# Up phase of a Strassen ConvFFN: weights in four places per pair, another product order, and the down weights' sums spread over all pairs

## The chip, the cores and the metric

One core of one Trainium2 chip runs the whole program. The metric is the device time of one execution in microseconds (us). TensorE (PE) multiplies, VectorE (DVE), ScalarE (ACT) and GpSimd (POOL) do the elementwise work, and SyncE (SP) issues nearly all transfers of the part that is changed, in program order.

## The reference

A decoder layer: three attention branches, a gated merge, and then a gated ConvFFN, which is where the change lies. All matrices are float32.

```
x = x + conv_ffn(rms_norm(x, norm2_g[l]), w_up[l], conv_w[l], conv_b[l], w_down[l])

def conv_ffn(h, w_up, conv_w, conv_b, w_down):
    a, b = jnp.split(h @ w_up, 2, axis=-1)
    a = lax.conv_general_dilated(a, conv_w..., padding=[(CONV_WIDTH - 1, 0)], ...) + conv_b
    return (jax.nn.gelu(a) * b) @ w_down
```

The sizes are: sequence 1024, model width 1024, D_FF 2816, so h @ w_up is 1024x1024 by 1024x5632, and the second product is 1024x2816 by 2816x1024.

## The kernel before

Both products of the ConvFFN are done with one level of the Strassen-Winograd scheme: a 2x2 block product in seven block products instead of eight, paid for with sums of the blocks. A product of fp32 accuracy is made of three matmuls (`mm3`: high by high on L283, low by high on L284, high by low on L285), so every operand is split into a rounded high part (a cast on ACT) and the rest (a subtraction on DVE).

**Up phase** (`ffn`). The 5632 columns are worked in 22 pairs s = 0 to 21; pair s takes 128 columns of the half a and the 128 columns of the half b that belong to them. The weights of a pair are four blocks of 128x512 elements: A11 and A12 (columns of a, upper and lower half of the rows), A21 and A22 (columns of b). A pair has seven products of 12 matmuls each, 84 matmuls of 128x512 (pair 0 has eight plain products; pair 1 has its own order, `EARLY`; all others go by `PRODUCTS`). Three sums of weights are made in place as soon as a pair's product S2 is prepared: su = A21 + A22 (L1400), S3 = A11 - A21 (L1402), S2 = su - A11 (L1404); S4 (L1407) follows later. They run on POOL, for pairs 0 and 1 on DVE. `prep` makes the sum if one is due, casts to the high part on ACT (L1411) and takes the low part on DVE (L1412; on POOL for pairs 0 and 1). Products are prepared three ahead (AHEAD) into a ring of four buffers ("wh" and "wl" in turn, two each). Every result comes out of PSUM through an add on DVE, goes through the convolution (`conv`: ACT L1465, two DVE steps L1470, ACT L1471) and is gated (`gated`, DVE L1475), and `left` and `sums` store the seven left operands of the second product to DRAM (L1430, L1440).

`load` brings a pair's weights as two transfers of 512 KB (L1384), one with A11 and A12, one with A21 and A22, into three buffers in rotation (two "wr", one "fr"). A buffer is free when every block in it, sums included, has been split.

`down_weights(k)`, for k = 0 to 10, is independent of all that: two loads of w_down (L1420, 512 KB each), four sums on POOL (L1421 to L1424) and two stores (L1426), in buffers "t2" that nothing else uses at that point. In the program it stands in pairs 1, 3, 5, ...; the scheduler of the framework sorts each engine's instructions by when their inputs are ready.

**Down phase** (`ffn_down`). Seven products of 11 blocks each; a block n is two loads (L1584, L1590), a cast of 128x1024 on ACT (L1592), a subtraction on DVE (L1593) and 12 matmuls. Blocks are loaded four ahead. Two of five blocks go through buffers of the long-lived pool wp, three of five through the pool dp. dp lies where the buffers of the up phase were, so its first loads wait until the last stores of the up phase have read theirs.

Of the kernel before, what the change touches and what calls it, by code (L numbers as in the profile page):

```python
# [13 lines left out]
P = 128  # L14
# [216 lines left out]
class Trunk:  # L231
# [1072 lines left out]
    PRODUCTS = (("A11", "B11"), ("S2", "T2"), ("A12", "B21"), ("S3", "T3"), ("A22", "T4"), ("S1", "T1"), ("S4", "B22"))  # L1304
# [62 lines left out]
    def ffn(self, np_, x1, B, blks):  # L1367
# [7 lines left out]
        cnt = {"raw": 0, "op": 0}  # L1375
        v, g = nc.vector.tensor_tensor, nc.gpsimd.tensor_tensor

        def load(s):
            pair, j = [], order[s]
            for c0 in (j * P, DFF + j * P):  # L1380
                pool, tag = (fp, "fr") if cnt["raw"] % 3 == 2 else (wp, "wr")
                cnt["raw"] += 1
                r = pool.tile([P, 8, P], F32, tag)
                nc.sync.dma_start(r, wup[:, c0:c0 + P].rearrange("(k p) n -> p k n", p=P))  # L1384
                pair.append(r)
            raws[s] = {"A11": pair[0][:, 0:4], "A12": pair[0][:, 4:8], "A21": pair[1][:, 0:4], "A22": pair[1][:, 4:8]}
# [4 lines left out]
        def prep(s, i):  # L1391

            if i == 0 and 0 < s < NF - 1:
                load(s + 1)
            q = raws[s]
            name = names(s)[i]
            e = g if s > 1 else v
            if name == ("S1" if s == 1 else "S2"):
                s1 = fp.tile([P, 4, P], F32, "su")
                e(s1, q["A21"], q["A22"], ALU.add)  # L1400
                q["S1"] = s1
                e(q["A21"], q["A11"], q["A21"], ALU.subtract)  # L1402
                q["S3"] = q["A21"]
                e(q["A11"], s1, q["A11"], ALU.subtract)  # L1404
                q["S2"] = q["A11"]
            if name == "S4":
                e(q["A12"], q["A12"], q["S2"], ALU.subtract)  # L1407
                q["S4"] = q["A12"]
            o = wp.tile([P, 2, 4, P], F32R, ("wh", "wl")[cnt["op"] % 2])
            cnt["op"] += 1  # L1410
            nc.scalar.copy(o[:, 0], q[name])  # L1411
            (v if s > 1 else g)(o[:, 1], q[name], o[:, 0].bitcast(F32), ALU.subtract)  # L1412
            ops[s, i] = o

        def down_weights(k):

            w = [np_.tile([P, 2, 512], F32, "t2") for _ in range(2)]
            for x in range(2):
                r = (k + x * NH) * P
                nc.sync.dma_start(w[x], wdn[r:r + P].rearrange("p (n c) -> p n c", n=2))  # L1420
            g(w[0][:, 1], w[0][:, 1], w[0][:, 0], ALU.subtract)  # L1421
            g(w[1][:, 1], w[1][:, 1], w[0][:, 1], ALU.subtract)
            g(w[0][:, 0], w[1][:, 1], w[0][:, 0], ALU.subtract)
            g(w[1][:, 0], w[1][:, 0], w[1][:, 1], ALU.subtract)  # L1424
            for x in range(2):
                nc.sync.dma_start(dt[k][:, 2 * x:2 * x + 2], w[x])  # L1426
# [22 lines left out]
        fp = Pool(self, "ffn", {"t1": 2})  # L1449
        load(1)  # L1450
        AHEAD = 3
        for s in range(NF):
# [51 lines left out]
            for i, (an, bn) in enumerate(self.EARLY if s == 1 else self.PRODUCTS):  # L1504
# [5 lines left out]
                if s % 2 == 1 and i == 4:  # L1510
                    down_weights(s // 2)
# [7 lines left out]
                elif s == 1:  # L1519
# [11 lines left out]
                    elif an == "S3":  # L1531
                        add(p1, p1)
                    else:
                        add(u2, p1)
                        gated(0, u2)
                        v(p1, p1, u3, ALU.add)
                        gated(1, p1)
                elif an == "S2":
                    add(u2, p1)
                elif an == "A12":  # L1540
                    add(p1, p1)
                    conv(0, p1)
                elif an == "S3":
                    add(u3, u2)
                elif an == "A22":
                    add(p1, u3)
                    gated(0, p1)
                elif an == "S1":
                    add(u2, u2)
                    add(u3, u3)  # L1550
                else:
                    add(u2, u2)
                    conv(1, u2)
                    gated(1, u3)
        sums(NH - 1)
        fp.close()
        np_.close()
        for p in blks:
            p.close()
        self.ffn_down(x1, dl, dt)  # L1560

    def ffn_down(self, x1, dl, dt):
# [4 lines left out]
        dp = Pool(self, "down", {"wr": 3, "wh": 3, "wl": 3, "st": 4})  # L1567
        rp = Pool(self, "downr", {"hi": NH, "lo": NH}, side="right")
        U = rp.tile([P, 4, 512], F32, "U")
        V = rp.tile([P, 4, 512], F32, "V")  # L1570
        fg = rp.tile([P, D], F32, "fg")
        nc.sync.dma_start(fg, a["final_g"].rearrange("(o d) -> o d", o=1).to_broadcast([P, D]))
        cnt = [0]

        def ring():
            cnt[0] += 1
            return wp if cnt[0] % 5 in (1, 2) else dp

        def operands(p, k, keep=None):

            an, bn = self.DOWN[p]
            pool = ring()
# [8 lines left out]
            hi, lo = ((keep or pool).tile([P, 2, 512], F32R, n) for n in (("hi", "lo") if keep else ("wh", "wl")))  # L1591
# [34 lines left out]
        ops = {n: operands(*seq[n]) for n in range(AHEAD)}  # L1626
        lasts = []
        lo_, hi_ = slice(0, 512), slice(512, 1024)
        for p in range(6):
            ps = [self.bank_tile() for _ in range(4)]  # L1630
            for k in range(NH):
                n = p * NH + k
                if n + AHEAD < len(seq):
                    ops[n + AHEAD] = operands(*seq[n + AHEAD])
# [3 lines left out]
                for t in range(4):  # L1638
                    step(ps[t], o, t, k == 0, k == NH - 1)
            for t in range(4):  # L1640
# [153 lines left out]
```

## Time and profile before

| What | Value |
|---|---|
| median of 3 runs | 1839.32 us (1835.39 to 1840.0) |
| profiled execution, its own time | 1841.05 us |
| span of that execution | 1839.3 us |
| mean granted clock of PE | 0.975 |
| PE busy | 1711.3 us (93%), 8600 matmuls |
| DVE busy | 1205.0 us (66%) |
| ACT busy | 770.8 us (42%) |
| POOL busy | 397.0 us (22%) |

The span is what the profiler saw of the program; the execution's own time lies 1.75 us above it. Matmuls are pipelined and their busy times overlap, so a PE that is shown busy is not yet at its best pace; the distance between starts tells the pace. The change touches the last third of the span.

### The profile page before, as it was taken

The numbers are of one execution on the slowest core, as the hardware profiler recorded it, in microseconds if no ns is written. First come the engines' busy times: TensorE is split into PE (matmuls) and PEld (weight loads), VectorE is DVE, ScalarE is ACT, GpSimd is POOL, SyncE is SP. The second block draws the span as 40 slices with busy tenths as digits, with TensorE's granted clock in tenths as the row PEclk, the third lists the DMA queues.
The fourth block names the chain that finished last, engine by engine and source line by source line (L and its number), as shares of the span: only waits on it lengthen the run. The fifth ranks groups of instructions, "written<-read, shape, count | busy, mean of one in ns | idle before, by whom it ended". The sixth has DMA issues, their size and how long they took to land. (4 is left out here: it accounts for less than half of the span.)

```text
span 1839.3 us, 24513 instructions
## 1 busy us (share of the span) xinstructions
PE 1711.3 (93%) x8600; PEld 1406.3 (76%) x8600; DVE 1205.0 (66%) x2518; ACT 770.8 (42%) x1572; POOL 397.0 (22%) x295
## 2 busy tenths in 40 slices
PE   7999999879899999999999997887999999879998
PEld 6888887768687888888877875666777777658876
DVE  7366676645567775666487179686868777745764
ACT  5335555432454534555554134222333333334452
POOL 4311101002111111111133207666332223100000
PEclk9999999989999999999999998998999999989999
DMA  8756566677425273221565402575532232467662
GB/s 256 205 138 159 145 155 181 159 197 199 111 77 157 70 183 93 77 64 47 187 202 193 152 4 83 177 235 174 182 96 87 93 108 86 130 214 229 211 208 74
DMA packets 223329, 266.49 MB, mean 145 GB/s; under 512 B 19720, under 2 KB 159086, under 8 KB 222998
## 3 DMA queue, kind: packets, MB, share of 16 engines
q1 hardware_dynamic: 214550, 246.94, 45.5%
q10 hardware_dynamic: 8208, 15.21, 2.3%
q0 software_dynamic: 448, 2.78, 0.4%
q8 instruction: 68, 1.11, 0.2%
q14 instruction: 55, 0.45, 0.1%
HBM read 187.23 MB, written 80.36 MB: 145 GB/s over the span
## 5 line engine op out<-in xcount | busy, mean ns | idle before, releaser
L283 PE MATMUL dn<-hTh,wh 128*128 128x512 f32 x704 | 285.7, 406 | 2.1 <-DVE sl L488 2.1
L285 PE MATMUL dn<-hTh,wl 128*128 128x512 f32 x704 | 277.3, 394 | 0.0
L284 PE MATMUL dn<-hTl,wh 128*128 128x512 f32 x704 | 276.9, 393 | 0.0
L271 POOL TENSOR_TENSOR wl<-wr,wh 128x1024 fp32r<-128x1024 f32 (+2 forms) x60 | 112.7, 1878 | 700.7 <-ACT wh L269 621.6
L712 ACT ACTIVATE p<-S,sm 128x384 f32<-128x384 f32 (+2 forms) x192 | 106.5, 559 | 138.3 <-DVE sm L708 103.8
L285 PEld LDWEIGHTS dn<-hTh,wl 128*128 128x128 f32 x704 | 133.1, 189 | 29.3
L283 PEld LDWEIGHTS dn<-hTh,wh 128*128 128x128 f32 x704 | 134.2, 191 | 20.8 <-DVE sl L488 2.5
L284 PEld LDWEIGHTS dn<-hTl,wh 128*128 128x128 f32 x704 | 134.0, 190 | 19.0
L776 DVE TENSOR_TENSOR tl<-T,th 128x512 fp32r<-128x512 f32 (+2 forms) x202 | 115.5, 585 | 33.9 <-ACT th L775 32.9
L704 DVE TENSOR_REDUCE sm<-S 128x1 f32<-128x384 f32 (+2 forms) x192 | 96.2, 525 | 52.6 <-PE S L701 51.7
L775 ACT CAST th<-T 128x512 fp32r<-128x512 f32 (+2 forms) x202 | 99.6, 510 | 67.5 <-PE T L769 64.7
L1593 DVE TENSOR_TENSOR wl<-wr,wh 128x1024 fp32r<-128x1024 f32 x66 | 80.2, 1223 | 63.0 <-ACT wh L1592 60.7
L701 PE MATMUL S<-k,q 114*128 114x384 f32 (+6 forms) x240 | 95.5, 398 | 16.3 <-issue 7.7
L1592 ACT CAST wh<-wr 128x1024 fp32r<-128x1024 f32 x66 | 69.3, 1053 | 95.8 <-PE dn L285 61.9
L798 PE MATMUL PV<-th,v 128*128 128x256 f32 (+1 forms) x362 | 94.0, 285 | 4.5 <-DVE yt L815 4.0
L769 PE MATMUL T<-ident,p 128*128 128x128 f32 x610 | 93.7, 275 | 2.2 <-DVE tl L776 2.1
L799 PE MATMUL PV<-tl,v 128*128 128x256 f32 (+1 forms) x362 | 89.3, 283 | 2.6 <-DVE tl L776 2.6
L697 PE MATMUL S<-k,q 128*128 128x384 f32 (+2 forms) x240 | 84.1, 350 | 6.8 <-DMA k<-dk_b 4.5
L769 PEld LDWEIGHTS T<-ident,p 128*128 128x128 f32 x610 | 72.8, 141 | 15.0 <-DVE tl L776 3.1
L798 PEld LDWEIGHTS PV<-th,v 128*128 128x128 f32 x362 | 69.1, 191 | 9.7 <-DVE yt L815 6.4
L799 PEld LDWEIGHTS PV<-tl,v 128*128 128x128 f32 x362 | 69.6, 192 | 6.2 <-DVE tl L776 3.7
L283 PE MATMUL S<-blk,wl 128*128 128x512 f32 x152 | 62.0, 408 | 12.2 <-ACT wl L1411 12.2
(463 smaller groups left out, 4451.4 us busy)
## 6 DMA issues: line engine op xcount, KB each, us to landing
wr<-w_in SPq DMA_DIRECT2D x44, 512.0 KB
wr<-dl SPq DMA_DIRECT2D x77, 256.0 KB
wr<-w_up SPq DMA_DIRECT2D x30, 512.0 KB
dg<-f ACTq DMA_DIRECT2D x48, 256.0 KB
gr<-dg SPq DMA_DIRECT2D x24, 512.0 KB
t<-w_down SPq DMA_DIRECT2D x22, 512.0 KB
dt<-t SPq DMA_DIRECT2D x22, 512.0 KB
wr<-dt SPq DMA_DIRECT2D x44, 256.0 KB
```

The lines of the kernel that those rows point to most:

```text
L271: eng.tensor_tensor(lo, raw, hi.bitcast(F32), ALU.subtract)
L283: nc.tensor.matmul(out, st[0], mv[0], start=first, stop=False)
L284: nc.tensor.matmul(out, st[0], mv[1], start=False, stop=False)
L285: nc.tensor.matmul(out, st[1], mv[0], start=False, stop=last)
L701: nc.tensor.matmul(ps[:, 0:wn * P], q[1][0:R, qs], k[1][0:R, cs], start=False, stop=True)
L704: nc.vector.tensor_reduce(mx if ci == 0 else sm[:, 1:2], v, AX.X, ALU.max, negate=True)
L712: nc.scalar.activation(pt[:, 0:m, :].rearrange("p a b -> p (a b)"), v, AF.Exp, bias=mx, accum_out=sm[:, 2 + ci:3 + ci])
L769: nc.tensor.transpose(ps[:, n * P:(n + 1) * P], b, self.ident)
L775: nc.scalar.copy(th[:, cs], ps[:, cs])
L776: nc.vector.tensor_tensor(tl[:, cs], ps[:, cs], th[:, cs].bitcast(F32), ALU.subtract)
L798: nc.tensor.matmul(unit.pv[:, oc], w, th[:, cs], start=first and i == 0, stop=False)
L799: nc.tensor.matmul(unit.pv[:, oc], w, tl[:, cs], start=False, stop=e)
```

## The change

The four weight blocks of a pair get places of their own. A11 and A12 have two sets of places in turn (half of the first "wr" buffer each for even pairs, half of "fr" each for odd pairs); A21 and A22 have one set (the second "wr" buffer) for all pairs. A load now brings one block (256 KB), so there are 88 loads of w_up instead of 44. A11 and A12 of the next pair are asked for when a pair's first product is prepared, A21 as soon as S3 (which sits in A21's place) is split, A22 as soon as A22 is split. The order of the products becomes A11, A12, S2, S3, A22, S1, S4 (A12 and S2 change places), and the partial results of a pair change tiles: what u3 held is in p1 and the reverse. `down_weights` stands in pairs 2, 3, 5, 6, 8, 10, 11, 13, 14, 16 and 18, and its two loads are tied to come after the last load of w_up that was issued before them. In the down phase, blocks 0 to 3 go through wp (block 2's split parts through "t2" buffers) before the buffers of the up phase are given up; blocks 4 to 7 are prepared at n = 3 instead of one at a time at n = 0 to 3; final_g is loaded into a tile made at n = 12.

```diff
-    PRODUCTS = (("A11", "B11"), ("S2", "T2"), ("A12", "B21"), ("S3", "T3"), ("A22", "T4"), ("S1", "T1"), ("S4", "B22"))
+    PRODUCTS = (("A11", "B11"), ("A12", "B21"), ("S2", "T2"), ("S3", "T3"), ("A22", "T4"), ("S1", "T1"), ("S4", "B22"))
...
-        def load(s):
-            pair, j = [], order[s]
-            for c0 in (j * P, DFF + j * P):
-                pool, tag = (fp, "fr") if cnt["raw"] % 3 == 2 else (wp, "wr")
-                cnt["raw"] += 1
-                r = pool.tile([P, 8, P], F32, tag)
-                nc.sync.dma_start(r, wup[:, c0:c0 + P].rearrange("(k p) n -> p k n", p=P))
...
+        place = lambda t, x: t[:, x * 4:x * 4 + 4]
+        raw = [wp.tile([P, 8, P], F32, "wr") for _ in range(2)]
+        SLOTS = {("A11", 0): place(raw[0], 0), ("A12", 0): place(raw[0], 1), ("A21", 0): place(raw[1], 0),
+                 ("A22", 0): place(raw[1], 1)}
+
+        def load(s, what=("A11", "A12", "A21", "A22")):
+            q = raws.setdefault(s, {})
+            for n in what:
+                r = q[n] = SLOTS[n, s % 2 if n[1] == "1" else 0]
+                k0, c0 = (512 if n[2] == "2" else 0), order[s] * P + (DFF if n[1] == "2" else 0)
+                self.upload = nc.sync.dma_start(r, wup[k0:k0 + 512, c0:c0 + P].rearrange("(k p) n -> p k n", p=P))
...
             if i == 0 and 0 < s < NF - 1:
-                load(s + 1)
+                load(s + 1, ("A11", "A12"))
...
             ops[s, i] = o
+            if 0 < s < NF - 1 and name in ("S3", "A22"):
+                load(s + 1, ("A21",) if name == "S3" else ("A22",))
...
-                nc.sync.dma_start(w[x], wdn[r:r + P].rearrange("p (n c) -> p n c", n=2))
+                with self.tc.issue_after(self.upload.ins):
+                    nc.sync.dma_start(w[x], wdn[r:r + P].rearrange("p (n c) -> p n c", n=2))
...
+        raw.append(fp.tile([P, 8, P], F32, "fr"))
+        SLOTS.update({("A11", 1): place(raw[2], 0), ("A12", 1): place(raw[2], 1)})
...
+        DOWN_AT = [2 + (8 * k) // 5 for k in range(NH)]
...
-                if s % 2 == 1 and i == 4:
-                    down_weights(s // 2)
+                if i == 4 and s in DOWN_AT:
+                    down_weights(DOWN_AT.index(s))
...
-            return wp if cnt[0] % 5 in (1, 2) else dp
+            return wp if cnt[0] % 5 in (4, 0) else dp
...
-            pool = ring()
+            pool = ring() if dp else wp
...
-        ops = {n: operands(*seq[n]) for n in range(AHEAD)}
+
+        ops = {n: operands(*seq[n], first=np_ if n == 2 else None) for n in range(AHEAD)}
...
-                if n + AHEAD < len(seq):
-                    ops[n + AHEAD] = operands(*seq[n + AHEAD])
+                if n >= 3:
+                    for m in range(max(AHEAD, n + 1 if n == 3 else n + AHEAD), min(n + AHEAD, len(seq) - 1) + 1):
+                        ops[m] = operands(*seq[m])
...
+                if n == 2:
+                    np_.close()
+                    for x in blks:
+                        x.close()
+                    dp = Pool(self, "down", {"wr": 3, "wh": 3, "wl": 3, "st": 4})
...
+                if n == 12:
+                    fg = rp.tile([P, D], F32, "fg")
+                    nc.sync.dma_start(fg, a["final_g"].rearrange("(o d) -> o d", o=1).to_broadcast([P, D]))
```

In the changed file the lines move: the weight sums are L1403, L1405, L1407 and L1410, the low part is L1415, the loads of w_up L1389, the down weights' loads, sums and stores L1426, L1427 to L1430 and L1432, the stores of left operands L1436 and L1446, the down phase's loads L1585 and L1591 and that of final_g L1654.

The first place is POOL in pair 1, where it makes the low parts (L1412) of that pair's products. Before:

```order
L1421 TENSOR_TENSOR t_2435_12058<-t_2435_12058 128x512
L1422 TENSOR_TENSOR t_2436_12059<-t_2436_12059,t_2435_12058 128x512
L1423 TENSOR_TENSOR t_2435_12058<-t_2436_12059,t_2435_12058 128x512
L1424 TENSOR_TENSOR t_2436_12059<-t_2436_12059 128x512
L1412 TENSOR_TENSOR wl_11962<-fr_11824,wl_11962 128x512
L1412 TENSOR_TENSOR wh_11969<-su_11965,wh_11969 128x512
L1412 TENSOR_TENSOR wl_11977<-fr_11824,wl_11977 128x512
```

And of the change at the same place:

```order
L1415 TENSOR_TENSOR wl_11963<-fr_11826,wl_11963 128x512
L1415 TENSOR_TENSOR wh_11970<-su_11966,wh_11970 128x512
L1415 TENSOR_TENSOR wl_11978<-fr_11826,wl_11978 128x512
L1415 TENSOR_TENSOR wh_11995<-fr_11826,wh_11995 128x512
L1415 TENSOR_TENSOR wl_12018<-wr_11518,wl_12018 128x512
L1415 TENSOR_TENSOR wh_12036<-wr_11518,wh_12036 128x512
L1403 TENSOR_TENSOR su_12096<-wr_11518 128x512
```

The four sums of down_weights(0) no longer stand ahead of pair 1's low parts; the first set on POOL now comes after pair 3's first three weight sums.

The second place is SP in the middle of the up phase, around one set of down weights. Before (an early stretch, with pair 3 at work: the second load of pair 4, the first of pair 5, and the down weights k = 4 and 5):

```order
L1420 DMA t_2631_13311<-w_down 128x1024
L1420 DMA t_2632_13312<-w_down 128x1024
L1384 DMA wr_12220<-w_up 128x8x128
L1426 DMA dt_2349_11510<-t_2631_13311 128x1024
L1426 DMA dt_2349_11510<-t_2632_13312 128x1024
L1384 DMA wr_12365<-w_up 128x8x128
L1420 DMA t_2680_13624<-w_down 128x1024
L1420 DMA t_2681_13625<-w_down 128x1024
```

And of the change, around the set k = 6, which stands in pair 11 (wr_11518 is the second "wr" buffer, with A21 and A22; fr_11826 and wr_11517 are the two sets of places of A11 and A12):

```order
L1389 DMA wr_11518<-w_up 128x4x128
L1389 DMA fr_11826<-w_up 128x4x128
L1389 DMA wr_11518<-w_up 128x4x128
L1389 DMA fr_11826<-w_up 128x4x128
L1426 DMA t_2657_13635<-w_down 128x1024
L1426 DMA t_2658_13636<-w_down 128x1024
L1436 DMA dl_2339_11500<-gb_13552 128x512
L1432 DMA dt_2351_11512<-t_2657_13635 128x1024
L1432 DMA dt_2351_11512<-t_2658_13636 128x1024
L1389 DMA wr_11517<-w_up 128x4x128
L1389 DMA wr_11518<-w_up 128x4x128 x2
```

The loads of the down weights are now behind A21 and A22 of pair 12 and A11 and A12 of pair 13, and their two stores stand ahead of A11 of pair 14 and of A21 and A22 of pair 13.

The third place is SP where the up phase hands over to the down phase. Before (blocks k of the left operands are dl_2334 for k = 0 to dl_2344 for k = 10):

```order
L1584 DMA wr_15396<-dl_2334_11495 128x512
L1430 DMA dl_2344_11505<-x_15102 128x512
L1430 DMA dl_2344_11505<-tt_15240 128x512
L1590 DMA wr_15396<-dt_2345_11506 128x512
L1584 DMA wr_15415<-dl_2344_11505 128x512
L1440 DMA dl_2344_11505<-gb_14951 128x1024
L1430 DMA dl_2344_11505<-x_15102 128x512
L1590 DMA wr_15415<-w_down 128x512
L1584 DMA wr_15491<-dl_2337_11498 128x512
L1590 DMA wr_15491<-w_down 128x512
L1584 DMA wr_15276<-dl_2336_11497 128x512
L1590 DMA wr_15276<-w_down 128x512
```

And of the change:

```order
L1436 DMA dl_2344_11505<-x_15115 128x512
L1436 DMA dl_2344_11505<-tt_15243 128x512
L1585 DMA wr_15371<-dl_2342_11503 128x512
L1591 DMA wr_15371<-w_down 128x512
L1585 DMA wr_15435<-dl_2334_11495 128x512
L1446 DMA dl_2344_11505<-gb_14962 128x1024
L1436 DMA dl_2344_11505<-x_15115 128x512
L1591 DMA wr_15435<-w_down 128x512
L1585 DMA wr_15454<-dl_2335_11496 128x512
L1591 DMA wr_15454<-w_down 128x512
L1585 DMA wr_15331<-dl_2338_11499 128x512
L1591 DMA wr_15331<-w_down 128x512
```

Before, the loads of block 2 (from dl_2336) come last here, behind three blocks that are used later. In the change blocks 0 to 3 have been asked for earlier; the loads of blocks 8, 11 and 12 (from dl_2342, dl_2334 and dl_2335) and the last stores of the up phase stand ahead of block 4's (from dl_2338).

## Rows read from the trace of the kernel before

**Rows 1.** What PE waited for, 1100 to 1840 us (line, releaser: total, times, longest).

```profile
PE S L283 <- ACT wh L1592: 17.1, 1, 17.1
PE S L283 <- ACT wl L1411: 12.2, 3, 8.3
...
PE PV L285 <- POOL wl L1412: 5.0, 1, 5.0
```

**Rows 2.** Timeline of PE: start, duration, engine, line, operation.

```profile
1132.79 0.39 PE L283 MATMUL S<-blk,wh 128*128 128x512 f32 x1
...
1343.47 0.39 PE L283 MATMUL PV<-blk,wl 128*128 128x512 f32 x1
...
1379.64 0.39 PE L285 MATMUL dn<-blk,wh 128*128 128x512 f32 x1
...
1599.42 0.39 PE L283 MATMUL S<-wh 128*128 128x512 f32 x1
```

**Rows 3.** ACT's copies of product A11 out of PSUM: pairs 2, 7 and 21.

```profile
1174.43 0.59 ACT L1518 COPY p<-T 128x512 f32<-128x512 f32 x1 [5.15 <-DVE x L1475]
...
1300.22 0.56 ACT L1518 COPY p<-dn 128x512 f32<-128x512 f32 x1
...
1584.79 0.56 ACT L1518 COPY p<-T 128x512 f32<-128x512 f32 x1
```

**Rows 4.** Busy time per window: length; PE, PEld, DVE, ACT, POOL; clock; DMA share; GB/s.

```profile
1132.79:1599.42 466.63, 426.07 (x1765) 336.95 (x1764) 349.74 (x466) 155.64 (x279) 186.18 (x134) 0.96 0.41 136
1174.43:1300.22 125.79, 102.82 (x408) 80.03 (x408) 92.60 (x109) 34.91 (x64) 72.61 (x50) 0.91 0.64 215
1300.22:1584.79 284.57, 275.49 (x1169) 219.16 (x1168) 214.47 (x309) 101.03 (x183) 79.66 (x60) 0.99 0.31 99
```

**Rows 5.** The line of the down weights' loads: instructions, durations in ns, first and last start.

```profile
L1420 SPq DMA_DIRECT2D t<-w_down x22: 328/336/1582, 1128.7 to 1297.1; - x22
```

**Rows 6.** What SP's queue waited for, 1130 to 1640 us.

```profile
SPq L1384 <- DVE wh L1412: 79.7, 15, 12.8
```

**Rows 7.** What POOL waited for, 1130 to 1640 us.

```profile
POOL su L1400 <- DMA wr<-w_up: 80.5, 9, 13.2
POOL su L1400 <- DMA fr<-w_up: 60.7, 6, 13.8
```

**Rows 8.** Timeline of POOL in pair 1 and in pair 4.

```profile
1141.52 1.71 POOL L1412 TENSOR_TENSOR wl<-fr,wl 128x512 fp32r<-128x512 f32 x1
1143.19 1.73 POOL L1412 TENSOR_TENSOR wh<-su,wh 128x512 fp32r<-128x512 f32 x1
...
1241.24 1.26 POOL L1400 TENSOR_TENSOR su<-fr 128x512 f32<-128x512 f32 x1 [5.17 <-DMA fr<-w_up]
```

**Rows 9.** Timeline of SP's queue: pair 4, and after the up phase.

```profile
1235.25 0.79 SPq L1384 DMA_DIRECT2D fr<-w_up  x1
...
1608.55 0.32 SPq L1440 DMA_DIRECT2D dl<-gb  x1
...
1613.76 0.32 SPq L1584 DMA_DIRECT2D wr<-dl  x1
```

**Rows 10.** Timeline of DVE beside POOL's instructions of pair 1.

```profile
1140.36 1.75 DVE L1402 TENSOR_TENSOR wr<-fr,wr 128x512 f32<-128x512 f32 x1
```

**Rows 11.** Groups by line and form, 1130 to 1600 us.

```profile
L1470 DVE SCALAR_TENSOR_TENSOR t<-u,ccols,t 128x512 f32<-128x512 f32 x42 | 41.2, 980 | 0.8
...
L1400 POOL TENSOR_TENSOR su<-wr 128x512 f32<-128x512 f32 x13 | 18.4, 1413 | 106.5 <-DMA wr<-w_up 80.5 <-DVE gb L1475 26.0
...
L1424 POOL TENSOR_TENSOR t<-t 128x512 f32<-128x512 f32 x11 | 18.2, 1651 | 0.0
```

**Rows 12.** Timeline of ACT after the up phase: the cast of block 2.

```profile
1621.05 1.04 ACT L1592 CAST wh<-wr 128x1024 fp32r<-128x1024 f32 x1 [8.57 <-DMA wr<-w_down]
```

**Rows 13.** Timeline of PE around the last long wait.

```profile
1604.66 0.39 PE L285 MATMUL dn<-wh,wl 128*128 128x512 f32 x1
1622.14 0.79 PE L283 MATMUL S<-wh 128*128 128x512 f32 x1 [17.09 <-ACT wh L1592]
```

More of the change, by code (lines that the diff above doesn't have):

```diff
@@ L1374, in ffn @@
         raws, ops, gs = {}, {}, {}
-        cnt = {"raw": 0, "op": 0}
+        cnt = {"op": 0}
         v, g = nc.vector.tensor_tensor, nc.gpsimd.tensor_tensor
-        def load(s):
-            pair, j = [], order[s]
-            for c0 in (j * P, DFF + j * P):
-                pool, tag = (fp, "fr") if cnt["raw"] % 3 == 2 else (wp, "wr")
-                cnt["raw"] += 1
-                r = pool.tile([P, 8, P], F32, tag)
-                nc.sync.dma_start(r, wup[:, c0:c0 + P].rearrange("(k p) n -> p k n", p=P))
-                pair.append(r)
-            raws[s] = {"A11": pair[0][:, 0:4], "A12": pair[0][:, 4:8], "A21": pair[1][:, 0:4], "A22": pair[1][:, 4:8]}
+        place = lambda t, x: t[:, x * 4:x * 4 + 4]
[8 more added lines that the diff above has]
+                self.upload = nc.sync.dma_start(r, wup[k0:k0 + 512, c0:c0 + P].rearrange("(k p) n -> p k n", p=P))
         def names(s):
@@ L1537, in ffn @@
                         gated(1, p1)
+                elif an == "A12":
+                    add(u3, p1)
+                    conv(0, u3)
                 elif an == "S2":
                     add(u2, p1)
-                elif an == "A12":
-                    add(p1, p1)
-                    conv(0, p1)
                 elif an == "S3":
-                    add(u3, u2)
+                    add(p1, u2)
                 elif an == "A22":
-                    add(p1, u3)
-                    gated(0, p1)
+                    add(u3, p1)
+                    gated(0, u3)
                 elif an == "S1":
                     add(u2, u2)
-                    add(u3, u3)
+                    add(p1, p1)
                 else:
@@ L1553, in ffn, with ffn_down @@
                     conv(1, u2)
-                    gated(1, u3)
+                    gated(1, p1)
         sums(NH - 1)
         fp.close()
[L1557 to L1562, printed above, removed]
+        self.ffn_down(x1, dl, dt, np_, blks)
+    def ffn_down(self, x1, dl, dt, np_, blks):
         nc, a, wp = self.nc, self.a, self.wp
@@ L1566, in ffn_down, with operands @@
         v = nc.vector.tensor_tensor
[L1567 to L1572, printed above, removed]
         cnt = [0]
+        dp = None
         def ring():
             cnt[0] += 1
-            return wp if cnt[0] % 5 in (1, 2) else dp
-        def operands(p, k, keep=None):
+            return wp if cnt[0] % 5 in (4, 0) else dp
+        def operands(p, k, keep=None, first=None):
             an, bn = self.DOWN[p]
-            pool = ring()
+            pool = ring() if dp else wp
             raw = pool.tile([P, 2, 512], F32, "wr")
@@ L1590, in operands @@
             nc.sync.dma_start(raw[:, 1], src)
-            hi, lo = ((keep or pool).tile([P, 2, 512], F32R, n) for n in (("hi", "lo") if keep else ("wh", "wl")))
+            hi, lo = ((keep or first or pool).tile([P, 2, 512], F32R, n)
+                      for n in (("hi", "lo") if keep else ("t2", "t2") if first else ("wh", "wl")))
             nc.scalar.copy(hi, raw)
@@ L1639, in ffn_down @@
                     step(ps[t], o, t, k == 0, k == NH - 1)
+                if n == 2:
[3 more added lines that the diff above has]
+                    dp = Pool(self, "down", {"wr": 3, "wh": 3, "wl": 3, "st": 4})
+                    rp = Pool(self, "downr", {"hi": NH, "lo": NH}, side="right")
+                    U = rp.tile([P, 4, 512], F32, "U")
+                    V = rp.tile([P, 4, 512], F32, "V")
+                if n == 12:
+                    fg = rp.tile([P, D], F32, "fg")
+                    nc.sync.dma_start(fg, a["final_g"].rearrange("(o d) -> o d", o=1).to_broadcast([P, D]))
             for t in range(4):
```

## The prediction

> **What bounds the kernel now.** I looked first at what PE waits for, since PE is busy 93% of the span. In the part that the change touches the list has three kinds of entry: one wait of 17.1 us on the cast L1592, right at the start of the down phase; many short ones on casts L1411 of the up phase (the worst 8.3 us); and one of 5.0 us on POOL's low part L1412 [rows 1].
>
> Next comes PE's own pace. From 1343.47 to 1379.64 us the timeline shows 159 matmuls in a row without a gap, 36.17 us for 158 steps: 0.2289 us each, 2.75 us for a product of 12, and 19.23 us for a pair of 84 [rows 2]. Pairs 1 to 21 are 147 products, so 1764 x 0.2289 = 403.8 us. They take from 1132.79 to 1599.42, 466.6 us [rows 2, 4]. The up phase therefore loses 62.8 us against PE's pace. Part of that is plain idling, part is a slower clock around it: the granted clock is 0.91 where the waits are dense and 0.99 where they are rare [rows 4].
>
> Where the 62.8 us lie is told by the copies of product A11. From pair 2 to pair 7 they are 125.79 us apart for five pairs, 25.2 us each: 29.6 us lost. From pair 7 to pair 21 it is 284.57 us for 14 pairs, 20.3 us each: 15.4 us lost [rows 3, 4]. The other 17.8 us lie in pairs 1 and 2 and behind the last copy, and most of those in pair 1, where POOL's 5.0 us wait stands [rows 1].
>
> What is late? POOL's first weight sum waits for w_up to land, 80.5 + 60.7 us in 15 waits [rows 7], and SP's load of w_up waits 79.7 us for a split on DVE, also 15 times [rows 6]. So the buffers come free too late: with three buffers for two loads per pair, a load waits until the last block of an older buffer, S4, is split, six products into its pair. Then it takes 6.0 us until POOL starts (issued at 1235.25, sum at 1241.24) [rows 8, 9], then three sums, a cast and a low part. The early pairs are worse because all 22 loads of the down weights are issued by 1297.1 us [rows 5]: their four sums and two stores stand between the pair's own steps on POOL and SP.
>
> **The change, part by part.**
>
> *Down weights out of pair 1.* POOL now starts pair 1's low parts without four sums ahead of them. They ended at about 1141.5 us, when the low part started, and PE waited 5.0 us for POOL's low part [rows 1, 8]. This wait goes, with the slow clock behind it. I leave 4.5 us of loss in pair 1: DVE still makes its weight sums there.
>
> *Four places.* In pair s, with PE at its pace and the pair starting at 0, S3 is split when the ring buffer of the product before pair s comes free: at 2 to 3 us. That issues A21 of the next pair; A22 follows one product later, at 5 to 6 us. With the 6.0 us of the row it has landed at 12; POOL's three sums, at 1.41 us for the first [rows 11], are done at 16. PE needs S2 of the next pair as its third product, at 19.2 + 5.5 = 24.7 us, and the cast and low part before it take 1.5 us. So there are 7 us of slack, in each pair, where there was a wait. A11 and A12 are asked for a pair earlier still and never matter; the 44 more issues cost SP about 0.4 us each, beside waits of 12.8 us at most that it has now. The new order (A12 before S2) is what moves S2 back by 2.75 us; without it the slack would be 4.
>
> *Down weights spread.* Their cover is the room on POOL and DVE. POOL needs 79.66 us in 14 pairs now, 5.7 per pair, and four sums more make about 12 in 19.2 [rows 4, 11]. DVE is closer. In the 14 late pairs it is busy 214.47 us, 15.3 per pair; in the five early ones 92.60 us, 18.5 per pair, with about seven sets of down sums among them (72.61 us of POOL instead of 5 x 5.7 = 28.5, at 4 x 1.65 = 6.6 per set) [rows 4, 11]. So a set costs DVE (18.5 - 15.3) x 5 / 7 = 2.3 us: it is slowed beside POOL, as where a subtraction of 128x512 takes 1.75 us beside POOL's 1.71 [rows 8, 10]. A pair with a set then needs 17.6 us of DVE. Seven of the 11 are even pairs, which also hold the five small steps of `sums`; against the mean that is 1.7 more, 19.3, right at the pace, with a lighter odd pair after or before. I charge 3.5 us for all of them. If this cover fails, it is the second rival.
>
> So the up phase keeps 4.5 + 3.5 = 8 of its 62.8 us, and 54.8 us go. The bounds from the rows are 62.8 (all goes) and 47.4 (the 15.4 us of the late pairs stay, because they are not due to loads).
>
> *First down blocks.* Before, blocks 0 and 1 run 1599.42 to 1604.9, and block 2 starts at 1622.14, because its load waits at 1613.76 for the last stores to have read the tiles that dp takes; 7.3 us later its cast starts at 1621.05 [rows 9, 12, 13]. PE loses 17.3 us. Now four blocks are ready, which covers PE until 10.9 us after the up phase's end. Then block 4 is due, and in SP's order its load stands behind those of blocks 8, 11 and 12. Block 12's load takes the buffer of block 8, so it waits until block 8 is split, whose split parts go where block 3's were, which PE frees only at 10.9. A cast (1.04 us [rows 12]) and a subtraction as long put that at 13.3 at the earliest, and at 17 if block 8's own load, behind stores such as the one at 1608.55 (9.1 after the end) [rows 9], lands late. Block 4's load is then issued at 14 to 18, its cast starts 6.0 to 7.3 us later, and PE 1.1 after that: 21 to 26 against the 10.9 when it was due. The stall is moved by two blocks, and stays at 10 to 15 us instead of 17.3. I take 4.5 us of gain, bounds 2 and 17.3.
>
> *final_g and the rotated ring* move nothing on the path: the last products and the output go as before. I allow 2 us either way.
>
> The sum: 54.8 + 4.5 = 59.3 us. The profiled execution took 1841.05, which gives 1781.7; it lay 1.7 us over the median of the runs, so for the median I say **1780**, with 1772 to 1789 for this case alone (the 4.5, 3.5 and 10 to 15 us being halved or doubled). Anything within 0.3%, 5.5 us, could not be told from no change.
>
> **The rivals.**
>
> *All of it goes (10%).* The up phase runs at PE's pace but for 2 us, and SP's order at the seam does no harm since blocks 8 and 12 come free earlier than I think: 60.8 + 17.3 = 78 us, 1761. For it: nothing in the trace makes block 8 late for certain. Against it: the order on SP, which is fixed.
>
> *DVE becomes the bound (13%).* In the pairs with a set and `sums` a POOL instruction holds a DVE one for as long as in pair 1 [rows 8, 10]: 1.75 us against the usual mean of 0.98 for such a step [rows 11], 0.77 each. A pair has eight POOL instructions, four of them counted already in the 15.3: 15.3 + 1.7 + 4 x 0.77 = 20.1, and 0.9 over the pace in seven pairs is 6 us. Each lag idles PE and brings slow clock; with 1 to 1.5 us of that per heavy pair it is some 15 us in all: 1795. It is decided by DVE's busy time, above 19.2 in the even pairs or not. Against it: the 18.5 us with 1.4 sets per pair.
> The Trainium skill, "SBUF — State Buffer", section "SBUF: two separate sides", says that DVE and GpSimd share a port pair that is locked for a whole instruction when the DVE one has two SBUF inputs and the GpSimd one reads SBUF, so one of them blocks fully. The 1.75 beside 1.71 us look like that. By that rule alone each of eight POOL instructions could cost DVE 1.3 to 1.65 us, some 26 us in such a pair, 7 over the pace, and 1829 in all, for which I leave 1 of the 13%; the 18.5 us measured in the early pairs, with ten POOL instructions each, speak against so much, since many of DVE's steps read PSUM.
>
> *Slower (3%).* One mechanism: SP's queue. A21 and A22 of the next pair are now asked for only one pair ahead, and the stores of down weights and left operands stand ahead of them. If a load is issued or lands more than the 7 us of slack too late in every pair, PE waits in every pair. It decides at 59.3 / 20 = 3 us beyond the slack, a load that reaches POOL 16 us after it was due instead of 6; then nothing is gained, and at 6 us beyond it the time is 1900. For it: SP waits up to 12.8 us for one thing today [rows 6]. Against: these waits are for just the splits that now come earlier.
>
> *No change (2%)*: the early loads only move the wait from loads to PE's ring of four, and the pairs stay at 20 to 25 us. The waits that the trace shows do not point to it [rows 6, 7].
>
> **How the numbers follow.** The forecast has 70%, the rivals 10, 13, 3 and 2; the last 2 are mixtures around 1810. The first three cases are all faster. The range 1767 to 1796 takes in the forecast's own and most of the second rival; left out are most of the first rival and all that is slower. Faster 95%, same 2%, slower 3%.
>
> **What would show it.** Right: product copies 19.2 to 19.5 us apart from pair 2 on; no POOL wait on w_up that is followed by one of PE; the loads of w_down from pair 2 to pair 18; PE's longest wait still on L1592 (or its new number), 10 to 15 us, four blocks after the up phase, with block 4's load behind block 12's. Wrong: DVE over 19 us in even pairs with PE waiting on low parts (second rival); PE waits on a POOL sum in each pair (slower); no wait over 5 us at the seam (first rival).

## The result and the profile after

The changed kernel takes 1782.79 us (median of 4 runs, 1780.19 to 1788.83) against 1837.36 us for the kernel before on the same chips: a ratio of 0.9709, with a 95% interval of 0.9677 to 0.974. The forecast was 1780. The profiled execution took 1781.89 us, its span is 1780.0 us, so 59.3 us less than the span of 1839.3 before.

The first part of the page of the changed kernel gives the busy time of each engine:

```profile
PE 1694.6 (95%) x8600; PEld 1400.0 (79%) x8600; DVE 1239.6 (70%) x2518; ACT 771.3 (43%) x1572; POOL 417.0 (23%) x295
```

The same matmuls, and 35 us more on DVE for the same number of instructions (2518): they last longer. The list of PE's waits from 1100 us on answers to [rows 1]:

```profile
PE S L283 <- ACT wh L1594: 11.1, 1, 11.1
...
PE PV L283 <- ACT wl L1414: 2.1, 1, 2.1
PE S L285 <- DVE wl L1415: 2.1, 2, 1.5
...
PE PV L285 <- POOL wl L1415: 0.5, 1, 0.5
```

In the kernel before, the list for the up phase has more rows than [rows 1] shows:

```profile
PE T L283 <- ACT wl L1411: 6.1, 2, 5.8
PE PV L283 <- ACT wl L1411: 5.1, 4, 1.9
PE T L283 <- ACT wh L1411: 5.1, 2, 4.9
...
PE dn L283 <- ACT wh L1411: 1.8, 2, 1.3
...
PE T L285 <- DVE wh L1412: 1.2, 1, 1.2
PE S L285 <- DVE wl L1412: 1.0, 1, 1.0
PE dn L285 <- DVE wh L1412: 0.9, 2, 0.5
PE PV L285 <- DVE wl L1412: 0.4, 1, 0.4
```

With the 12.2 us of [rows 1], the waits on casts were 30.3 us; they are down to 2.1. POOL's 5.0 is down to 0.5, and the stall at the head of the down phase is 11.1 instead of 17.1. What stays are short waits on low parts from DVE: 3.6 us in all, 3.5 before. The windows of the up phase, whole and for three neighbouring pairs (8, 9 and 10, from one copy of product A11 to the next), have the columns of [rows 4]:

```profile
1130.08:1544.38 414.30, 407.98 (x1765) 331.23 (x1764) 387.34 (x467) 157.39 (x280) 206.35 (x134) 1.00 0.46 155
...
1280.14:1301.69 21.55, 21.55 (x95) 17.41 (x94) 21.45 (x24) 7.29 (x13) 13.00 (x8) 1.00 0.48 177
1301.69:1318.54 16.85, 16.85 (x75) 13.84 (x74) 15.45 (x20) 7.29 (x13) 6.18 (x4) 1.00 0.47 133
1318.54:1340.09 21.55, 21.55 (x96) 17.65 (x95) 21.44 (x24) 7.29 (x13) 12.99 (x8) 1.00 0.48 179
```

The up phase takes 414.3 us; 403.8 are PE's own pace, so 10.5 of the 62.8 us of loss are left, and the clock is full. But DVE is busy 387 of the 414 us (350 of 467 before), and in the two even pairs shown, which hold a set of down sums and the steps of `sums`, 21.4 of 21.5. The copies come 21.55 and 16.85 us apart in turn while PE never stops (busy for the whole of each of these windows): DVE falls behind in one pair and catches up in the next, and the results that wait in the PSUM banks between PE and DVE take up the difference (argued from these rows, not tested). From pair 2 to pair 21 the copies are 16.9 to 22.9 us apart, 19.5 in the mean.

The seam, in PE's timeline, SP's and ACT's:

```profile
1544.38 0.39 PE L283 MATMUL S<-wh 128*128 128x512 f32 x1
...
1555.83 0.39 PE L285 MATMUL dn<-wh,wl 128*128 128x512 f32 x1
1567.33 0.79 PE L283 MATMUL S<-wh 128*128 128x512 f32 x1 [11.11 <-ACT wh L1594]
```

```profile
1559.17 0.32 SPq L1585 DMA_DIRECT2D wr<-dl  x1
...
1560.01 0.43 SPq L1585 DMA_DIRECT2D wr<-dl  x1
```

```profile
1556.84 1.04 ACT L1594 CAST wh<-wr 128x1024 fp32r<-128x1024 f32 x1 [2.40 <-DMA wr<-w_down]
1566.24 1.04 ACT L1594 CAST wh<-wr 128x1024 fp32r<-128x1024 f32 x1 [8.35 <-DMA wr<-w_down]
```

The up phase ends at 1544.38. Block 8 is cast at 1556.84, block 12's load follows at 1559.17, block 4's at 1560.01 (15.6 us after the end), its cast at 1566.24, and PE goes on at 1567.33, 22.95 us after the end. Before it was 22.72 us [rows 2, 13], but with two blocks done instead of four.

So the 59.3 us of the span are: 2.7 before pair 1's first product (1130.08 instead of 1132.79 us, in work that the change does not touch), 52.3 in the up phase, 5.2 at the seam (two blocks, 5.4, less 0.2), and 0.9 lost after it.

### The profile page after: what moved, and what is told of

Its sections match the earlier page's. It is cut to its first block, busy times and chain, and to the rows that moved or that the text cites. A ratio compares the mean times of both kernels' runs of the same rounds, so it can differ in the third digit from the quotient of the medians.

```text
span 1780.0 us, 24605 instructions
## 1 busy us (share of the span) xinstructions
PE 1694.6 (95%) x8600; PEld 1400.0 (79%) x8600; DVE 1239.6 (70%) x2518; ACT 771.3 (43%) x1572; POOL 417.0 (23%) x295
## 4 chain that ended last, share of the span: by engine, by line
PE 29%; DVE 16%; issue 5%; DMA 5%; ACT 3%; POOL 3%; SPq 0%; DVEq 0%; POOLq 0%; ACTq 0%
PE dn L285 5%; PE dn L283 5%; PE dn L284 5%; DVE t L1479 3%; DVE u L1525 3%; DVE wl L1415 2%; DMA gr<-dg 2%; PE S L285 2%; PE S L284 2%; PE S L283 2%; DVE wh L1415 2%; PE T L769 1%; DVE x L1484 1%; PE T L285 1%; PE T L284 1%
## 5 line engine op out<-in xcount | busy, mean ns | idle before, releaser
L1479 DVE SCALAR_TENSOR_TENSOR t<-u,ccols,t 128x511 f32<-128x511 f32 (+1 forms) x88 | 97.7, 1110 | 7.3 <-ACT t L1474 6.2
```

The costliest lines, as they stand in the source:

```text
L1479: nc.vector.scalar_tensor_tensor(o, i, cw[2 - sh], o, ALU.mult, ALU.add)
```

## The experiments

Twelve kernels were run. This table gives for each the median, the ratio to the kernel before on the same chip, and from its profile the length of the up phase, its loss against 403.8 us, DVE's busy time in it, and PE's longest wait at the seam. The last four columns are read from one profiled execution each; those of runs 2 and 3 took 4.4 us more than their medians, those of runs 6 and 9 took 3.5 and 4.6 us less. Runs 4 and 7 have the changed kernel's up phase, and runs 8 and 11 share one; their losses still differ by up to 4.0 us, so a smaller difference in that column says nothing unless a wait in the trace goes with it. The intervals of runs 4, 5, 7, 8, 11 and 12 overlap that of the changed kernel; what separates these runs from it are the medians and the traces.

| Run | Median us | Ratio, 95% interval | Up phase | Loss | DVE busy | Seam |
|---|---|---|---|---|---|---|
| before | 1837.36 | 1 | 466.6 | 62.8 | 349.7 | 17.1 |
| changed | 1782.79 | 0.9709 (0.9677 to 0.974) | 414.3 | 10.5 | 387.3 | 11.1 |
| 1 spread only | 1837.48 | 0.9997 (0.998 to 1.0013) | 464.4 | 60.6 | 336.1 | 15.8 |
| 2 places only | 1808.31 | 0.9845 (0.983 to 0.986) | 444.5 | 40.7 | 371.2 | 10.7 |
| 3 old order | 1797.85 | 0.9779 (0.9763 to 0.9796) | 430.0 | 26.2 | 372.9 | 11.5 |
| 4 old seam | 1788.13 | 0.9729 (0.9715 to 0.9744) | 412.5 | 8.7 | 385.5 | 16.5 |
| 5 no down sums | 1776.25 | 0.9664 (0.964 to 0.9689) | 408.3 | 4.5 | 346.2 | 11.1 |
| 6 sums twice | 1837.36 | 0.9987 (0.9972 to 1.0002) | 465.0 | 61.2 | 409.8 | 10.9 |
| 7 seam through wp | 1776.49 | 0.9668 (0.9641 to 0.9694) | 413.0 | 9.2 | 383.7 | 5.4 |
| 8 odd pairs | 1780.10 | 0.9683 (0.9653 to 0.9712) | 412.8 | 9.0 | 387.4 | 10.6 |
| 9 before, no sums | 1809.63 | 0.9847 (0.983 to 0.9864) | 433.7 | 29.9 | 321.3 | 15.7 |
| 10 sums on DVE | 1795.53 | 0.9774 (0.9756 to 0.9792) | 423.1 | 19.3 | 374.2 | 11.2 |
| 11 runs 7 and 8 together | 1774.29 | 0.9665 (0.9648 to 0.9683) | 408.8 | 5.0 | 386.5 | 5.8 |
| 12 late sums on DVE | 1778.23 | 0.9669 (0.9651 to 0.9687) | 408.2 | 4.4 | 369.2 | 11.2 |

**Run 1: the spread alone**, on the kernel before.

```diff
-                if s % 2 == 1 and i == 4:
-                    down_weights(s // 2)
+                if i == 4 and s in DOWN_AT:
+                    down_weights(DOWN_AT.index(s))
...
+                with self.tc.issue_after(self.upload.ins):
+                    nc.sync.dma_start(w[x], wdn[r:r + P].rearrange("p (n c) -> p n c", n=2))
```

> The kernel before, with its three weight buffers and its product order, and only the down weights moved to the eleven pairs 2 to 18 and tied behind the last load of w_up. Theory (the prediction's sum): the buffers that come free late cost about 1.1 us in every pair, and the down weights standing between the pair's own steps cost the rest (29.6 - 5 x 1.1 = 24 us in pairs 2 to 6, some 8 in pair 1). So 25 to 32 us faster than before, about 1808, with some 23 us of loss left in the up phase. Rival 1 (buffers alone are the cause): under 8 us faster. Rival 2 (the spread is all): 50 us or more faster.

It gave nothing: 0.9997. The expected 25 to 32 us fell. ACT's copies of pairs 2 and 17 show what happened:

```profile
1162.59 0.59 ACT L1520 COPY p<-T 128x512 f32<-128x512 f32 x1 [1.86 <-DVE x L1477]
...
1495.69 0.57 ACT L1520 COPY p<-S 128x512 f32<-128x512 f32 x1
```

That is 333.1 us for 15 pairs, 22.2 each, where it was 25.2 in the early pairs and 20.3 in the late ones [rows 3]. The loss was spread with the sums, not removed.

**Run 2: four places, order and seam, without the spread.**

```diff
-                with self.tc.issue_after(self.upload.ins):
-                    nc.sync.dma_start(...)
+                nc.sync.dma_start(...)
...
-                if i == 4 and s in DOWN_AT:
-                    down_weights(DOWN_AT.index(s))
+                if s % 2 == 1 and i == 4:
+                    down_weights(s // 2)
```

> The changed kernel, with the down weights back in the odd pairs and without the tie, so that they are issued early again; four places, product order and the new first down blocks stay. Theory: the late pairs gain 15 us and the seam 5, the early pairs stay slow because POOL and SP still do the down weights there: 20 to 35 us faster than before, about 1810. Rival 1 (four places alone cure the up phase, since the loads now come early enough for the disturbance): about 1783, as the changed kernel. Rival 2 (places are worth nothing without the spread): only the seam's 5 us.

1808.31, as the theory had it. All down-weight loads are issued by 1290.0 us again (1297.1 before), and all of PE's waits over 0.3 us in the up phase lie ahead of 1284 us; 40.7 us of loss are left. From 1351.15 to 1562.64 us, the last eleven steps from one copy of A11 to the next, a pair takes 19.2 us, which is PE's own pace. So once the early sums are done, the places and the new order together leave nothing of the 1.1 us that a late pair lost before.

**Run 3: the old order of the products.**

```diff
-    PRODUCTS = (("A11", "B11"), ("A12", "B21"), ("S2", "T2"), ...
+    PRODUCTS = (("A11", "B11"), ("S2", "T2"), ("A12", "B21"), ...
...
```

The partial results go back to their old tiles as well.

> The changed kernel with the old order of products (S2 second, A12 third) and the partial results back in their old tiles. Theory: S2 is needed 2.75 us earlier, which takes 3 of some 7 us of slack: within 4 us of the changed kernel. Rival (the slack is already used up): PE waits 2 us or more on S2 in each pair, 20 to 55 us slower than the changed kernel.

15 us slower than the changed kernel; 26.2 us of loss. Less than the rival said, but not the 4 us of the theory. PE waits for low parts from DVE, and DVE for a cast. Ahead of pair 9, in order of time:

```profile
1295.70 0.68 DVE L1415 TENSOR_TENSOR wh<-fr,wh 128x512 fp32r<-128x512 f32 x1
1296.30 0.68 DVE L1525 TENSOR_TENSOR p<-S,u 128x512 f32<-128x512 f32 x1
...
1296.52 1.30 POOL L1407 TENSOR_TENSOR fr<-su,fr 128x512 f32<-128x512 f32 x1 [3.34 <-DVE wh L1415]
...
1297.86 0.62 ACT L1414 CAST wl<-fr 128x512 fp32r<-128x512 f32 x1 [1.95 <-POOL fr L1407]
...
1298.51 1.78 DVE L1415 TENSOR_TENSOR wl<-fr,wl 128x512 fp32r<-128x512 f32 x1 [1.53 <-ACT wl L1414]
```

S2 is written in the place of A11, so POOL's sum waits until DVE has taken A11's low part (1295.70). With S2 as the very next product, DVE has only one add left to do until the sum (1.30 us) and the cast (0.62 us) are through, and it stands still for 1.53 us. This wait is in the trace 19 times, once in each pair from 3 to 21, 29.0 us in all. In the changed kernel, where A12 comes between, DVE waits for such a cast five times after pair 1, 3.3 us in all. So the order is worth about 15 us, and the trace names this link; a kernel with this link alone changed was not run.

**Run 4: the old first down blocks** (the up phase's buffers given up before block 0, all blocks through the ring, `ffn_down` as it was).

> The changed kernel with the first down blocks as before (blocks 0 to 3 through the ring, the buffers of the up phase given up before block 0). Theory: the stall is back at 17 us after two blocks, 5 us slower than the changed kernel. Rival (the stall was only moved by two blocks): within 1.5 us of the changed kernel.

5.3 us slower by the medians, and PE's wait is 16.5 us after two blocks: the theory.

**Runs 5 and 6: the down sums left out, and made twice.**

```diff
-            g(w[0][:, 1], w[0][:, 1], w[0][:, 0], ALU.subtract)
-            g(w[1][:, 1], w[1][:, 1], w[0][:, 1], ALU.subtract)
-            g(w[0][:, 0], w[1][:, 1], w[0][:, 0], ALU.subtract)
-            g(w[1][:, 0], w[1][:, 0], w[1][:, 1], ALU.subtract)
```

> The changed kernel without the four POOL sums of each down-weight set; the rows of w_down are stored as they were loaded (this leaves out part of the computation). In the changed kernel DVE is busy 387 of the 414 us of the up phase and PE loses 10.5 us there. Theory (DVE's steps are held up by POOL's): DVE's busy time in the up phase falls by about 25 us (2.3 per set), and the whole gets 3 to 6 us faster. Rival (DVE is busy with its own work, POOL does not matter): DVE's time stays within 5 us and so does the whole within 1 us.

> The changed kernel with the four POOL sums of each set made twice in a row (44 more POOL instructions, about 72 us of POOL; the values stored change). Theory (a POOL instruction holds up DVE, and DVE is nearly the bound): DVE's busy time grows by about 25 us, PE gets waits on low parts in the seven even pairs with a set, 8 to 25 us slower than the changed kernel. Rival (POOL has the room, 206 of 414 us, and DVE is not touched): within 2 us.

Without the sums (the stored weights are then the loaded ones) the kernel is 6.5 us faster, and the up phase's window is

```profile
1130.27:1538.53 408.26, 405.69 (x1765) 332.17 (x1764) 346.24 (x466) 165.00 (x279) 131.28 (x90) 1.00 0.47 157
```

DVE does the same instructions in 346.2 instead of 387.3 us, and PE has no wait over 0.3 us on a low part from DVE. So 44 instructions of POOL, 75 us of its time, cost DVE 41 us: 3.7 us per set, 0.93 per instruction. The rival that DVE is not touched is out.

Twice as many made it 55 us slower, over twice what the theory allowed. PE's waits are nearly all of one kind:

```profile
PE dn L285 <- DVE wh L1415: 8.7, 5, 3.2
PE S L285 <- DVE wl L1415: 8.0, 10, 1.7
PE T L285 <- DVE wl L1415: 7.1, 7, 1.7
```

DVE is busy 22.5 us longer, near the 25 of the theory, but that is 409.8 of 465.0 us: DVE is not full. In pair 9, which has no set, it is busy 15.5 of 20.4 us:

```profile
1321.65:1342.05 20.40, 18.74 (x79) 14.27 (x78) 15.51 (x20) 7.29 (x13) 9.29 (x7) 1.00 0.42 130
```

What it waits for is seen ahead of pair 12, on SP, POOL, ACT and DVE in turn:

```profile
1367.23 2.02 SPq L1436 DMA_DIRECT2D dt<-t  x2
1369.34 1.34 SPq L1389 DMA_DIRECT2D wr<-w_up  x2
...
1375.40 1.29 POOL L1403 TENSOR_TENSOR su<-wr 128x512 f32<-128x512 f32 x1 [6.51 <-DMA wr<-w_up]
...
1379.47 0.62 ACT L1414 CAST wl<-wr 128x512 fp32r<-128x512 f32 x1 [7.49 <-POOL wr L1407]
...
1380.12 1.10 DVE L1415 TENSOR_TENSOR wl<-wr,wl 128x512 fp32r<-128x512 f32 x1 [4.49 <-ACT wl L1414]
```

The two stores of a set stand in SP's queue until POOL has made the sums, and the loads of w_up stand behind them. POOL's weight sums then start late, the cast of S2 comes late, and DVE stands still for 4.49 us. Over the phase, first SP and DVE of this run, then SP of the changed kernel:

```profile
SPq L1436 <- POOL t L1433: 111.6, 11, 10.6
DVE wl L1415 <- ACT wl L1414: 28.0, 7, 4.5
...
SPq L1432 <- POOL t L1429: 67.7, 11, 7.1
```

So the doubled sums cost in two ways, DVE's longer steps and the loads held back on SP. How the 55 us divide between the two was not tested.

**Run 7: blocks 4 and 5 through wp.**

```diff
-            return wp if cnt[0] % 5 in (4, 0) else dp
+            return wp if cnt[0] % 5 in (1, 2) else dp
```

> The changed kernel with blocks 4 and 5 of the down phase, instead of 7 and 8, in the long-lived pool wp (the ring's two numbers are 1 and 2 instead of 4 and 0). Theory: block 4 is then loaded where block 7 is now, its cast starts about 9 us after the end of the up phase, in time; the stall moves to block 6, which is due at 16.4 us and comes at about 23: 6 us instead of 11.1, so 4 to 6 us faster than the changed kernel. Rival (the whole stall moves on because block 6's load starts later too): within 1.5 us.

6.3 us faster than the changed kernel by the medians. The one long wait left at the seam, 5.4 us instead of 11.1, stands before block 6:

```profile
1566.48 0.80 PE L283 MATMUL S<-wh 128*128 128x512 f32 x1 [5.36 <-ACT wh L1594]
```

**Run 8: sets in odd pairs.**

```diff
-        DOWN_AT = [2 + (8 * k) // 5 for k in range(NH)]
+        DOWN_AT = [2, *range(3, 20, 2), 20]
```

> The changed kernel with the down weights in pairs 2, 3, 5, 7, 9, 11, 13, 15, 17, 19 and 20, so that only two of the eleven sets lie in even pairs, which also hold the steps of the left operands' sums. Theory (what PE loses after pair 1 comes from DVE being full in even pairs with a set): DVE's load evens out, 2 to 4 us faster. Rival (these losses are single events, and DVE's backlog is evened out by the eight PSUM banks anyway): within 1.5 us.

2.7 us faster by the medians, but its interval overlaps that of the changed kernel, and DVE's total is the same. Runs 4 and 7, whose up phase is that of the changed kernel, lose 8.7 and 9.2 us there, so 9.0 does not stand out. Inconclusive.

**Run 9: the kernel before without the down sums** (the same four lines left out).

> The kernel before without the four POOL sums of each down-weight set (part of the computation is left out); its loads, stores, buffers and order stay. Theory A (formed after the spread alone gave nothing): the buffers that come free late are what costs, and the sums only decide in which pairs: 5 to 15 us faster than before, with 45 us or more of the 62.8 us of loss still there. Theory B (the prediction's split): some 30 us of the loss go, since the early pairs are then like the late ones.

26.6 us faster by the medians, near the 30 of theory B. Theory A, formed after run 1, fell here. Of the 62.8 us of loss, 29.9 stay without the sums and 32.9 go with them, 3.0 per set; by the medians it is 2.4 per set.

**Runs 10 and 12: the down sums on DVE**, in the same place, and half a pair later.

```diff
-            g(w[0][:, 1], w[0][:, 1], w[0][:, 0], ALU.subtract)
+            v(w[0][:, 1], w[0][:, 1], w[0][:, 0], ALU.subtract)
...
```

In run 12 they are also taken out of `down_weights`:

```diff
+        def down_sums():
+            k, w = fetched.pop()
+            with self.tc.issue_after(self.low.ins):
+                v(w[0][:, 1], w[0][:, 1], w[0][:, 0], ALU.subtract)
...
+                if i == 1 and s - 1 in DOWN_AT:
+                    down_sums()
```

> The changed kernel with the four sums of each down-weight set on DVE instead of POOL. Theory (a POOL instruction holds DVE up): without these sums DVE was busy 346 us in the up phase, with them on POOL 387, that is 0.93 us for each of 44; on DVE a step of 128x512 takes 0.68, so 44 add only 30: DVE at about 376, less than with the sums on POOL, and the whole is 0 to 4 us faster. Rival (DVE is simply full, and work given to it makes it slower): 8 us or more slower.

> As the run with the four sums of each set on DVE, but the first of them is tied behind a low part of the following pair, about half a pair later, so that the rows of w_down have landed when DVE comes to them. Theory (DVE's time falls when the sums leave POOL, and only its wait of 17.8 us for w_down made that run slower): DVE at about 375 us in the up phase with no wait on w_down, up phase 410 to 414 us, 0 to 4 us faster than the changed kernel. Rival (44 more instructions on DVE hold up the low parts behind them wherever they stand): up phase 420 us or more, 8 us or more slower than the changed kernel, as before.

Run 10 had DVE's busy time as the theory (374.2 us) and the total as the rival (12.7 us slower than the changed kernel). What DVE waits for in its up phase explains the contradiction:

```profile
DVE t L1427 <- DMA t<-w_down: 17.8, 11, 2.8
```

In each of the eleven sets DVE stands still until the rows of w_down land, and all low parts behind stand with it. In run 12, with the sums half a pair later, that wait is gone, and the window reads

```profile
1129.72:1537.93 408.21, 405.91 (x1766) 332.28 (x1764) 369.20 (x509) 164.49 (x279) 135.95 (x89) 1.00 0.46 157
```

DVE does 44 instructions more than in the changed kernel and is busy 18 us less; 4.4 us of loss are left, as without the sums. The whole is 4.6 us faster than the changed kernel by the medians, 0.9669 against 0.9709. The move also shortens SP's waits before the stores of the sums, from 67.7 to 24.5 us; what that gives by itself was not tested.

**Run 11: runs 7 and 8 together.**

> The changed kernel with both: blocks 4 and 5 through wp, and the down weights in pairs 2, 3, 5, 7, 9, 11, 13, 15, 17, 19 and 20. Theory: the two gains lie in different stretches and add, 6.3 + 2.7 = 9 us faster than the changed kernel, about 1774. Rival: what the up phase saves is lost at the seam, as the last sums come closer to it: about 1777.

1774.29 us, 8.5 under the changed kernel, near the 9 that the two gains would add up to. But it is only 2.2 us under run 7 alone, and the up phase that it shares with run 8 lost 5.0 us here and 9.0 there, so what the odd pairs give stays open. It is the fastest kernel that was run; it was not combined with run 12.

## Why the prediction was right

The forecast sum of 59.3 us is that of the profiled spans to the tenth, and that is luck: 2.7 of the measured 59.3 us lie ahead of the up phase, in work that the change does not touch, and by the medians the gain is 54.6 us. What carries the prediction are its two parts, the up phase (54.8 forecast, 52.3 measured) and the seam (4.5 and 5.2).

**The up phase** was to keep 8 of 62.8 us and kept 10.5. The mechanism, late buffers cured by earlier loads with slack for the rest, is borne out by runs 2 and 9. That loads were late is in the trace of the kernel before as well: from 1343 to 1560 us, eleven pairs, DVE stood still for 42.0 us until the cast of S2 was made. Nine of these waits are 2.6 to 5.6 us long, behind POOL sums that had waited for w_up [rows 7]; two are 1.5 us, as in run 3:

```profile
DVE wh L1412 <- ACT wh L1411: 23.6, 6, 4.6
DVE wl L1412 <- ACT wl L1411: 18.4, 5, 5.6
```

In run 9, without the sums, the old buffers and order still lose 29.9 us; in run 2 the places and the new order bring the late pairs to PE's pace, while 40.7 us stay in the pairs with early sums. The sign "product copies 19.2 to 19.5 us apart" held in the mean (19.5) and not for the single pairs (16.9 to 22.9).

**Pair 1** was to keep 4.5 us. Runs 5 and 12, where PE's waits over 0.3 us in the up phase lie in pair 1 alone, lose 4.5 and 4.4 us in all. POOL's wait fell from 5.0 to 0.5 us.

**The spread's price** was mis-sized. The term was 2.3 us of DVE per set, and 3.5 us for PE in all; measured are 3.7 us per set (run 5 against the changed kernel) and 6.0 us for PE (10.5 less 4.5; 4.2 and 4.7 with the losses of runs 4 and 7). The 2.3 came from five early pairs against 14 late ones, and the early pairs held long waits, in which POOL's sums ran while DVE had nothing to do (argued, not tested).

**The second rival** came half true. Its condition, DVE over 19.2 us in even pairs with PE waiting on low parts, is met: 21.4 us, and 3.6 us of such waits, though the kernel before had 3.5. Its price, 15 us, is not, since the odd pairs catch up. Run 6, where the change's whole gain is gone, is this rival and the one called "slower" together: DVE is busy 22.5 us longer, and stands still for 28.0 us because the stores of the sums hold back the loads on SP.

**The product order** was the step that failed. I took the load's slack without it as 4 of 7 us, so costless; run 3 lost 15 us. I had looked at when the weights land. What run 3 shows instead is that S2 is written over A11: with S2 right behind A11, DVE stands still for 1.5 us in each pair, 29.0 us in all, until the sum and the cast are made.

**The seam** went as worked out: a stall of 11.1 us (10 to 15 forecast), block 4's load behind block 12's, at 15.6 us (14 to 18), PE at 22.95 (21 to 26); 5.2 us of gain for 4.5. Run 4 gives 5.3 by itself, and run 7 shows that the place of blocks 4 and 5 kept 5.7 of the 11.1 us that were left.

**What joins the parts.** The halves of the change in the up phase do not simply add. The spread alone takes 2.2 us off the loss (run 1), the places and the order alone 22.1 (run 2), both together 52.3. A set of down sums cost 2.4 to 3.0 us where the pairs were already late (run 9 against before), and run 1 shows that moving the sets within such pairs gains nothing; it costs 0.4 to 0.55 us (4.2 to 6.0 over 11) where the pairs have slack.

How POOL costs DVE is seen in the timeline of pair 8 in the changed kernel, DVE first, then POOL:

```profile
1294.15 0.68 DVE L1525 TENSOR_TENSOR u<-T,u 128x512 f32<-128x512 f32 x1
1294.75 1.19 DVE L1415 TENSOR_TENSOR wl<-wr,wl 128x512 fp32r<-128x512 f32 x1
1295.86 3.49 DVE L1479 SCALAR_TENSOR_TENSOR t<-u,ccols,t 128x512 f32<-128x512 f32 x2
1299.27 1.78 DVE L1415 TENSOR_TENSOR wh<-wr,wh 128x512 fp32r<-128x512 f32 x1
1300.98 0.68 DVE L1484 TENSOR_TENSOR gb<-t,p 128x512 f32<-128x512 f32 x1
```

```profile
1293.56 1.83 POOL L1427 TENSOR_TENSOR t<-t 128x512 f32<-128x512 f32 x1
1295.46 1.64 POOL L1428 TENSOR_TENSOR t<-t,t 128x512 f32<-128x512 f32 x1
1297.18 1.62 POOL L1429 TENSOR_TENSOR t<-t,t 128x512 f32<-128x512 f32 x1
1298.76 1.75 POOL L1430 TENSOR_TENSOR t<-t 128x512 f32<-128x512 f32 x1
```

The add that reads PSUM (L1525) takes its 0.68 us while POOL's first sum runs. The steps that read two operands of SBUF take 1.19 to 1.78 us, in time with POOL's; the last, after POOL is done, 0.68 again.
The Trainium skill, "SBUF — State Buffer", section "SBUF: two separate sides", names as the DVE instructions that contend for the locked port pair those in a 2-port mode and those with two SBUF inputs, the latter only against a GpSimd one that reads SBUF. The trace agrees with this for the second kind: the steps with two SBUF operands are the ones that get longer. The average of 0.93 us per POOL instruction of 1.7 us (75 us for 44) is less than a full block of each.

## What to carry to other kernels

A POOL instruction is not free because POOL has room: here each took 0.93 us of DVE's time, more than the 0.68 us that the same step took on DVE itself once its input had landed. Weigh an instruction in an in-order queue by what it waits for as well: the same sums on DVE were 12.7 us slower behind a load and 4.6 us faster by the medians half a pair later. A result that is written over an operand makes a chain through that operand's last reader; put other work between the two, as A12 between A11 and S2. And before two changes are judged alone, ask whether one of them makes the slack that the other needs.

## What was unexpected of the hardware

DVE's slowdown beside POOL is selective and both ways: 128x512 steps with two SBUF operands went from 0.68 us to between 1.2 and 1.8 us, adds from PSUM stayed at 0.68, and POOL's own sums were slowed from 1.26 us [rows 8] to 1.62 to 1.83 us. That 44 instructions moved from POOL to DVE made DVE's total fall from 387.3 to 369.2 us was worked out beforehand (375), but more than expected.
